# Gate vectors kept as columns and spread by transposes; matmul operands placed at one offset; 12 modulation chunks moved to VectorE

## The chip, the cores and the metric

The kernel runs on one core of one Trainium2 chip. The metric is device time in microseconds (us); lower is better. TensorE (PE in the profile) multiplies, VectorE (DVE) and ScalarE (ACT) work element by element, GpSimd (POOL) does a few powers, SyncE's queue (SP) starts most transfers. On-chip operands lie in SBUF, matmul results in PSUM.

## The reference, cut to what matters

Two streams of 128 tokens (a context stream, s = 0, and a latent stream, s = 1; width 2048) go through two layers. A layer computes six modulation vectors of 2048 from a conditioning vector, with a 2048 x 12288 weight matrix, and uses them around attention and a squared-ReLU MLP:

```python
sh_a, sc_a, gt_a, sh_m, sc_m, gt_m = split(silu(c) @ w_ada[l] + b_ada[l], 6)
h = rms_norm(x, g_pre_a) * (1.0 + sc_a) + sh_a
o = attention_heads(h @ w_in[l]) @ w_out[l]
x = x + gt_a * rms_norm(o, g_post_a)
h = rms_norm(x, g_pre_m) * (1.0 + sc_m) + sh_m
x = x + gt_m * rms_norm(square(relu(h @ w_up[l])) @ w_down[l], g_post_m)
```

Everything is float32. The weights are about 590 MB, read once. Both streams use the same weights; their modulation vectors differ.

## The kernel before, in words

**Weights and their split.** Weights come in chunks of 1 MB ([128, 2048] floats) into five `raw` buffers. For a matmul of the trunk ("t" chunk: w_in, w_out, w_up, w_down) each half of a chunk is split into a high part `wh` (ACT, L1031) and a low part `wl` (DVE, L1032, `split_to`), with three buffers each, two halves ahead of use. The activations are split likewise. Each product is then three matmuls in the fast 32-bit form: high by high, low by high, high by low. In `Group` (L364 to L366: w_in, w_out, w_down) the activation is stationary and 512 weight columns move; in `UpGroup` (L399 to L401: w_up, 128 chunks in all, 48 matmuls each) the weight is stationary and 256 activation columns move. Four PSUM accumulators are shared by both. The stationary activation is `XT0` to `XT3` for w_in and `big` for w_out and w_down.

**Modulation chunks.** The modulation weights are 1 MB chunks too, in one of two layouts. "ada" chunks go to TensorE (`ada_mm`, L150: four matmuls by 32 columns at once, each as two instructions); four chunks make one block of 512 outputs, which ACT copies (L154), TensorE transposes (L121, four of them on the tile `pt`) and DVE reduces (L167). "dv" chunks go to VectorE (`dv_mul`, L205): two products with a broadcast copy of silu(c), one for each stream (`sB`), each with a running sum of 2048 elements; four chunks make a block. The tables `DV_BLOCKS` and `PE_BLOCKS` say which blocks go where: before, layer 0 has 4 blocks on VectorE (the MLP gate, `G_M`) and 18 blocks, and two more in halves, on TensorE: 80 chunks, all in the first stage (w_in and w_out of layer 0, about 0 to 505 us). The 64 dv chunks that run beside the MLP of layer 0 and the 28 later ones make the 92 of the profile.

**Order.** `items` is a list written by the program: trunk chunks, with ada and dv chunks woven between them (`weave`). SP starts the transfers in about that order, as `raw` buffers come free (`issue`, L1018); a scheduler then orders each engine's instructions and may move one ahead of others that the program wrote earlier, unless `behind` forbids it. In the trace before, DVE takes dv products ahead of low parts written before them, and waits for their transfers.

**Gates.** A finished gate block (16 in all: two gates, two layers, four blocks) goes through `gate_fin`: it is written into a 32-column tile `gt`, four matmuls (L234, eight instructions) turn its columns into rows, ACT and DVE split these into `gc`. When a gate is needed, `gate_bc` spreads a block over 128 partitions by one matmul with a selector (`sv`, L301). It is called 32 times: two gates, two layers, two streams, four blocks; ACT (L879) or DVE (L954) reads the result.

**Addresses.** A pool lays its tiles out one behind the other, in the order in which their names are first asked for. `const` comes first, then `wp` (`raw`, `wh`, `wl`: all of 4 or 8 KB), then `sp`, which begins with five `big` of 8 KB, then `cT` of 128 bytes, then `tmp` (2 KB), `XT0` to `XT3` (8 KB each), small tiles, `stg`. So `raw`, `wh`, `wl` and `big` have one offset within 2 KB, and `XT` lies 128 bytes further.

Of the kernel before, what the change touches and what calls it, by code (L numbers as in the profile page):

```python
# [29 lines left out]
NACC = 4  # L30
TAIL = 4


G_A, G_M = [(2, b) for b in range(4)], [(5, b) for b in range(4)]
M_A = [(i, f) for f in range(4) for i in range(2)]
M_M = [(3 + i, f) for f in range(4) for i in range(2)]
DV_BLOCKS = [G_M, M_A + M_M[:4] + G_A[:3] + G_M]
PE_BLOCKS = [M_A[2:] + G_A + M_M, M_M[4:] + G_A[3:]]

C_ID, C_GC, C_GS, C_DC, C_DS, C_MK, C_LO, C_SV, C_END = 0, 128, 256, 384, 448, 512, 576, 577, 833


def _consts():
    c = np.zeros((P, C_END), np.float32)
    c[:, C_ID:C_ID + P] = np.eye(P, dtype=np.float32)
    for g in range(4):
        for v in range(2):  # L50
            for r in (v, 2 + v):
                c[32 * g + r, C_SV + P * v:C_SV + P * (v + 1)] = 1.0
            c[32 * g + 2 + v, C_LO] = -1.0
# [19 lines left out]
def trunk(ctx: ExitStack, tc: tile.TileContext, I, O):  # L73
    nc = tc.nc
    pe, act, dve, pool = nc.tensor, nc.scalar, nc.vector, nc.gpsimd

    const = ctx.enter_context(tc.tile_pool(name="const", bufs=1))
    wp = ctx.enter_context(tc.tile_pool(name="wp", bufs=1))
    sp = ctx.enter_context(tc.tile_pool(name="sp", bufs=1))
# [3 lines left out]
    def sb(shape, tag, bufs=1, dt=F32):  # L83
        return sp.tile(shape, dt, tag=tag, bufs=bufs, name=tag)

    def psm():
        return ps.tile([P, 512], F32, tag="m", bufs=7 - NACC, name="m")

    cs = const.tile([P, C_SV], F32, name="cs")
    ident = cs[:, C_ID:C_ID + P]  # L90
    sv = const.tile([P, 2 * P], F32R, name="sv")
    x = [None, None]
    xd = [I["xp"], I["xs"]]
    sT = const.tile([P, KT, 32], F32, name="sT")
    baT = const.tile([P, L, 96], F32, name="baT")
    ngT = const.tile([P, L, 4, KT], F32, name="ngT")
    hf = const.tile([P, 8], F32, name="hf")
    mods = [[const.tile([P, KT, 2], F32, name=f"mod{l}_{i}") for i in range(4)] for l in range(L)]
    biasB = const.tile([P, 4, P], F32, name="biasB")
# [17 lines left out]

    mark = {"pt": None, "res": None, "xt": None}

# [3 lines left out]
    def startup():  # L123
        for s in range(2):
            x[s] = sb([P, D], "big", 5)
            nc.sync.dma_start(x[s], xd[s])
        cT = sb([P, 2, KT], "cT")
        nc.scalar.dma_start(cT, I["cT"])
        nc.scalar.dma_start(cs, I["consts"][:, 0:C_SV])
        svf = sb([P, 512], "tmp", NTMP)  # L130
        nc.scalar.dma_start(svf[:, 0:2 * P], I["consts"][:, C_SV:C_END])
        nc.scalar.dma_start(baT, I["baT"])
        nc.scalar.dma_start(ngT, I["ngT"])
        dve.memset(sT, 0.0)
        dve.memset(hf, -0.5)
        for v in range(2):
            act.activation(sT[:, :, v], cT[:, v, :], AF.Silu)
        act.activation(sv, svf[:, 0:2 * P], AF.Copy)

# [16 lines left out]

    gcs = {}
    made = set()

    def ada_post(l, sec, blk, pt, j0, nj):  # L160
        yield
        m = psm()
        for j in range(nj):
            tr(m[:, j * P:(j + 1) * P], pt[:, j * P:(j + 1) * P])
        yield
        red = st1[:, 0:2 * nj].rearrange("p (j v) -> p j v", v=2)
        dve.tensor_reduce(red, m[:, 0:nj * P].rearrange("p (j g c) -> p j c g", g=4, c=32)[:, :, 0:2, :], AX.X,  # L167
                          ALU.add)
        if sec in (2, 5):
            yield from gate_fin(l, sec, blk, red)  # L170
        else:
            mod_fin(l, sec, blk, red, j0, nj)
# [20 lines left out]
    def load_sb():  # L193
        for v in range(2):
            nc.sync.dma_start(sB[v], I["crow"][v:v + 1, :].to_broadcast([P, D]))
        for v in range(2):
            act.activation(sB[v], sB[v], AF.Silu)

    def dv_mul(l, sec, blk, j, raw, release):
# [3 lines left out]
        for v in range(2):  # L203
            o = raw if v else sb([P, D], "junk", 1, FP8)
            p = dve.scalar_tensor_tensor(o, raw, 1.0, sB[v], ALU.mult, ALU.mult, accum_out=a[:, j, v:v + 1],  # L205
                                         saturate=None if v else False)
            behind(p, mark["xt"])
            if v:
                release()
            yield  # L210
        if j == 3:
            if sec in (2, 5):
                yield from gate_fin(l, sec, blk, a)
            else:
                mod_fin(l, sec, blk, a)

    def gate_fin(l, sec, blk, red):

        w = 0 if sec == 2 else 1
        gt = sb([P, 4, 32], "gt")  # L220
        dve.memset(gt, 0.0)
        k0 = 4 * blk
        for v in range(2):
            dve.tensor_tensor(gt[:, :, v], red[:, :, v], baT[:, l, 16 * sec + k0:16 * sec + k0 + 4], ALU.add)
            dve.tensor_tensor(gt[:, :, v], gt[:, :, v], ngT[:, l, 2 * w + 1, k0:k0 + 4], ALU.mult)
        dve.tensor_copy(gt[:, :, 2:4], gt[:, :, 0:2])
        if (l, w) not in gcs:
            gcs[(l, w)] = sb([P, 512], "gc", dt=F32R)
        gc = gcs[(l, w)]
        yield  # L230
        m = psm()
        r = slice(32 * blk, 32 * blk + 32)
        for j in range(4):
            pe.matmul(m[r, j * P:(j + 1) * P], gt[:, j, :], ident, start=True, stop=True,  # L234
                      tile_position=(0, 32 * blk))
        yield
        h = sb([P, 512], "tmp", NTMP, F32R)
        act.activation(h[r, :], m[r, :], AF.Copy)
        dve.scalar_tensor_tensor(gc[r, :], h[r, :].bitcast(F32), cs[r, C_LO:C_LO + 1], m[r, :], ALU.mult, ALU.add)
        made.add((l, w, blk))  # L240
# [54 lines left out]

    def gate_bc(l, w, s, n):
        m = psm()
        gc = gcs[(l, w)]
        assert (l, w, n) in made
        r = slice(32 * n, 32 * n + 32)  # L300
        pe.matmul(m, sv[r, P * s:P * (s + 1)], gc[r, :], start=True, stop=True,  # L301
                  tile_position=(32 * n, 0))
        return m
# [482 lines left out]
    for l in range(L):  # L786
# [41 lines left out]
        if l == 0:  # L828
            items.insert(0, ("call", startup))
            fill, dv = ada_items(0, G_A + M_M), []  # L830
            h0 = lambda h: [("ada", I["w_ada0"][sec, h, kq], (0, sec, 0, kq, h)) for sec in range(2) for kq in range(4)]
# [9 lines left out]
            items.extend(a1[:2] + m[3:4] + a1[2:4] + m[4:5] + a1[4:6] + m[5:6] + a1[6:] + m[6:7])  # L841
            xt(1)
            items.extend(m[7:])
            for f in range(1, 4):
                ch = [c for cg in cG for c in cg[2 * f:2 * f + 2]]
                if f == 1:
                    call(lambda l=l: layer_consts(l))
                if f < 3:
                    weave(ch[:5], ada_items(0, M_A[2 * f + 2:2 * f + 4]))
                    items.append(ch[5])  # L850
                    xt(f + 1)
                    items.extend(ch[6:])
                else:
                    weave(ch, fill[:8])
            weave(c2, fill[8:16])
            rest, fill = [], fill[16:]
        else:
# [165 lines left out]
    def split_to(k):  # L1023
        while state["split"] <= min(k, len(subs) - 1):
# [136 lines left out]
```

## Time and profile before

| what | us |
|---|---|
| median of 3 runs (2336.02 to 2344.62) | 2338.56 |
| the profiled execution's own time | 2343.01 |
| its span, first to last instruction | 2340.9 |
| PE busy, of the span | 2272.9 |
| DVE busy | 1613.8 |
| ACT busy | 1100.9 |

The profiled execution is one run with a profile; durations are read from it. PE rows are matmuls as the profile models their ends: consecutive ones overlap, so the rate is read from the distance between starts, not from the duration of one. PEclk in the profile is the granted clock, a share of full speed.

### The profile page before, as it was taken

How to read it: one execution, taken by the hardware profiler on the slowest of the kernel's cores; microseconds unless marked ns; L12 is line 12 of the kernel's file. 1: busy time of each engine (PE TensorE's matmuls, PEld its weight loads, DVE VectorE, ACT ScalarE, POOL GpSimd, SP SyncE). 2: the span in 40 equal slices, each digit the busy share in tenths (PEclk: the TensorE clock that was granted, in tenths of full speed). 3: DMA queues.
4: the chain of work that ended last, by engine and by line, in shares of the span. 5: the costliest groups of instructions: out<-in, count | busy, mean ns of one | idle time of the engine just before them, and what ended most of it. 6: DMA issues, size and time to landing. Idle time of an engine off the chain costs nothing.

```text
span 2340.9 us, 33080 instructions
## 1 busy us (share of the span) xinstructions
PE 2272.9 (97%) x13480; PEld 1901.3 (81%) x13480; DVE 1613.8 (69%) x2028; ACT 1100.9 (47%) x1525; POOL 21.8 (1%) x30
## 2 busy tenths in 40 slices
PE   6999999989999999999999999998999999999998
PEld 3567666779889889889877777877989988988986
DVE  2565755489888998998758688547566566565545
ACT  4334444465444445435445455546544444543543
POOL 0000000000000000000000000000000000000000
PEclk9999999999999999999999999999999999999999
DMA  8888777887877777787857665665666566565552
GB/s 325 301 321 335 289 302 303 338 285 294 307 273 296 291 290 289 275 298 279 338 185 274 247 242 197 240 241 209 216 232 220 200 230 216 201 223 210 192 183 90
DMA packets 92496, 601.35 MB, mean 257 GB/s; under 512 B 13752, under 2 KB 16184, under 8 KB 21432
## 3 DMA queue, kind: packets, MB, share of 16 engines
q1 hardware_dynamic: 91624, 598.64, 69.2%
q8 instruction: 105, 1.72, 0.3%
q10 hardware_dynamic: 720, 0.61, 0.1%
q14 instruction: 47, 0.39, 0.0%
HBM read 591.61 MB, written 7.60 MB: 256 GB/s over the span
## 4 chain that ended last, share of the span: by engine, by line
PE 87%; DVE 6%; DMA 2%; issue 2%; ACT 2%; POOL 1%; ACTq 0%; POOLq 0%; DVEq 0%
PE acc L364 16%; PE acc L365 16%; PE acc L366 16%; PE acc L401 10%; PE acc L400 10%; PE acc L399 10%; PE ada L150 4%; DVE wl L1032 3%; PE m L121 2%; DMA raw<-w_adaT_in 2%; PE m L487 1%; PE m L234 1%; POOL st L108 1%; DMA raw<-w_in_in 0%; DVE raw L205 0%
## 5 line engine op out<-in xcount | busy, mean ns | idle before, releaser
L1031 ACT ACTIVATE wh<-raw 128x1024 fp32r<-128x1024 f32 x720 | 759.0, 1059 | 918.0 <-PE acc L366 548.6
L1032 DVE TENSOR_TENSOR wl<-raw,wh 128x1024 fp32r<-128x1024 f32 x720 | 874.7, 1223 | 418.7 <-ACT wh L1031 416.3
L401 PE MATMUL acc<-XT,wl 128*128 128x256 f32 x2048 | 580.3, 284 | 2.5 <-DVE wl L1032 2.5
L399 PE MATMUL acc<-XT,wh 128*128 128x256 f32 x2048 | 577.3, 282 | 2.5 <-ACT XT L277 2.5
L400 PE MATMUL acc<-XT,wh 128*128 128x256 f32 x2048 | 579.4, 283 | 0.3 <-DVE XT L278 0.3
L364 PE MATMUL acc<-wh,big 128*128 128x512 f32 x1280 | 502.0, 394 | 0.0
L365 PE MATMUL acc<-wl,big 128*128 128x512 f32 x1280 | 500.2, 391 | 1.7 <-DVE wl L1032 1.7
L366 PE MATMUL acc<-wh,big 128*128 128x512 f32 x1280 | 498.7, 390 | 0.0
L399 PEld LDWEIGHTS acc<-XT,wh 128*128 128x128 f32 x2048 | 387.5, 189 | 4.0 <-ACT XT L277 3.1
L401 PEld LDWEIGHTS acc<-XT,wl 128*128 128x128 f32 x2048 | 386.5, 189 | 3.8 <-DVE wl L1032 3.6
L400 PEld LDWEIGHTS acc<-XT,wh 128*128 128x128 f32 x2048 | 386.0, 188 | 0.8 <-DVE XT L278 0.5
L364 PEld LDWEIGHTS acc<-wh,big 128*128 128x128 f32 x1280 | 240.1, 188 | 61.5 <-issue 9.2
L365 PEld LDWEIGHTS acc<-wl,big 128*128 128x128 f32 x1280 | 240.5, 188 | 52.0 <-DVE wl L1032 3.4
L366 PEld LDWEIGHTS acc<-wh,big 128*128 128x128 f32 x1280 | 240.4, 188 | 50.5 <-issue 0.5
L364 PE MATMUL acc<-wh,XT 128*128 128x512 f32 x576 | 230.6, 411 | 9.9 <-ACT wh L1031 6.5
L205 DVE SCALAR_TENSOR_TENSOR junk<-raw,sB 128x2048 fp8e5<-128x2048 f32 x92 | 210.5, 2288 | 36.5 <-DMA raw<-w_adaT_in 36.4
L365 PE MATMUL acc<-wl,XT 128*128 128x512 f32 x576 | 229.7, 399 | 1.6 <-DVE wl L1032 1.2
L366 PE MATMUL acc<-wh,XT 128*128 128x512 f32 x576 | 228.0, 396 | 0.0
L205 DVE SCALAR_TENSOR_TENSOR raw<-raw,sB 128x2048 f32<-128x2048 f32 x92 | 210.4, 2287 | 0.0
L364 PEld LDWEIGHTS acc<-wh,XT 128*128 128x128 f32 x576 | 108.5, 190 | 51.1 <-ACT wh L1031 12.2
L365 PEld LDWEIGHTS acc<-wl,XT 128*128 128x128 f32 x576 | 109.0, 189 | 31.3 <-DVE wl L1032 6.5
L366 PEld LDWEIGHTS acc<-wh,XT 128*128 128x128 f32 x576 | 108.8, 189 | 24.5 <-issue 0.2
(134 smaller groups left out, 1225.1 us busy)
## 6 DMA issues: line engine op xcount, KB each, us to landing
raw<-w_up_in SPq DMA_DIRECT2D x128, 1024.0 KB, 5.6
raw<-w_down_in SPq DMA_DIRECT2D x128, 1024.0 KB, 5.0
raw<-w_adaT_in SPq DMA_DIRECT2D x92, 1024.0 KB, 4.9
raw<-w_ada_in SPq DMA_DIRECT2D x80, 1024.0 KB, 6.3
raw<-w_in_in SPq DMA_DIRECT2D x72, 1024.0 KB, 5.8
raw<-w_out_in SPq DMA_DIRECT2D x32, 1024.0 KB, 4.8
XT<-w_ada_in SPq DMA_DIRECT2D x12, 1024.0 KB, 7.4
raw<-w_ada_in SPq DMA_DIRECT2D x16, 512.0 KB, 5.1
```

The costliest lines, as they stand in the source:

```text
L108: pool.tensor_tensor(out, out, hf[:, 0:width], ALU.pow)
L121: pe.transpose(out, in_, ident)
L150: pe.matmul(pa[32 * g:32 * g + 32, 0:w], sT[:, 4 * kq + g, :], raw[:, g * w:(g + 1) * w], start=(kq == 0), stop=(kq == 3), tile_position=( ...
L205: p = dve.scalar_tensor_tensor(o, raw, 1.0, sB[v], ALU.mult, ALU.mult, accum_out=a[:, j, v:v + 1], saturate=None if v else False)
L364: pe.matmul(a, xh, wh[:, c], start=first, stop=False)
L365: pe.matmul(a, xh, wl[:, c], start=False, stop=False)
L366: pe.matmul(a, xl, wh[:, c], start=False, stop=last)
L399: pe.matmul(a, wh[:, c], xh, start=first, stop=False)
L400: pe.matmul(a, wh[:, c], xl, start=False, stop=False)
L401: pe.matmul(a, wl[:, c], xh, start=False, stop=last)
L1031: act.activation(wh, r, AF.Copy)
L1032: behind(dve.tensor_tensor(wl, r, wh.bitcast(F32), ALU.subtract), mark["res"])
```

## The change

Three parts, in the words of the code. Gates: `gate_fin` writes a block into the columns of one `gates[w]` tile, [128, 16, 2], with two additions and two products and nothing on TensorE; `gate_bc` makes four transposes (L121's helper) of one such column, repeated 128 times by a step of zero. `gt`, `gc`, `sv`, the selector constants and their copy at the start are gone. Addresses: a pool `lead` (512 bytes and three times 128) stands first, then `wp`, then a new pool `op` with `big`, `XT`, `stg` and `tmp`, then the constants, then the rest. Chunks: blocks G_A[0], G_A[1] and the last of M_M of layer 0 (12 chunks) become dv chunks in the first stage; `sB` is loaded there, and every dv product and every low part, in both layers, is chained behind the one written before it.

```diff
+OPERANDS = ("big", "XT0", "XT1", "XT2", "XT3", "stg", "tmp")
-DV_BLOCKS = [G_M, M_A + M_M[:4] + G_A[:3] + G_M]
-PE_BLOCKS = [M_A[2:] + G_A + M_M, M_M[4:] + G_A[3:]]
+DV_BLOCKS = [G_A[:2] + M_M[7:] + G_M, M_A + M_M[:4] + G_A[:3] + G_M]
+PE_BLOCKS = [M_A[2:] + G_A[2:] + M_M[:7], M_M[4:] + G_A[3:]]
...
+    lead = ctx.enter_context(tc.tile_pool(name="lead", bufs=1))
+    wp = ctx.enter_context(tc.tile_pool(name="wp", bufs=1))
+    op = ctx.enter_context(tc.tile_pool(name="op", bufs=1))
     const = ctx.enter_context(tc.tile_pool(name="const", bufs=1))
-    wp = ctx.enter_context(tc.tile_pool(name="wp", bufs=1))
     sp = ctx.enter_context(tc.tile_pool(name="sp", bufs=1))
...
-        return sp.tile(shape, dt, tag=tag, bufs=bufs, name=tag)
+        pl = op if tag in OPERANDS else sp
+        return pl.tile(shape, dt, tag=tag, bufs=bufs, name=tag)
...
-    ngT = const.tile([P, L, 4, KT], F32, name="ngT")
+    ngT = lead.tile([P, L, 4, KT], F32, name="ngT")
-    mods = [[const.tile([P, KT, 2], F32, name=f"mod{l}_{i}") for i in range(4)] for l in range(L)]
+    mods = [[(lead if 4 * l + i < 3 else const).tile([P, KT, 2], F32, name=f"mod{l}_{i}") for i in range(4)]
+            for l in range(L)]
...
+    def chain(inst):
+        behind(inst, mark["dve"])
+        mark["dve"] = inst
...
-        nc.scalar.dma_start(cs, I["consts"][:, 0:C_SV])
-        svf = sb([P, 512], "tmp", NTMP)
-        nc.scalar.dma_start(svf[:, 0:2 * P], I["consts"][:, C_SV:C_END])
+        nc.scalar.dma_start(cs, I["consts"])
...
-        act.activation(sv, svf[:, 0:2 * P], AF.Copy)
...
+    gates = [const.tile([P, KT, 2], F32, name=f"gate{w}") for w in range(2)]
...
     def load_sb():
         for v in range(2):
             nc.sync.dma_start(sB[v], I["crow"][v:v + 1, :].to_broadcast([P, D]))
+
+    def silu_sb():
         for v in range(2):
-            act.activation(sB[v], sB[v], AF.Silu)
+            behind(act.activation(sB[v], sB[v], AF.Silu), mark["wh"])
...
             behind(p, mark["xt"])
+            chain(p)
...
     def gate_fin(l, sec, blk, red):
         w = 0 if sec == 2 else 1
-        gt = sb([P, 4, 32], "gt")
-        dve.memset(gt, 0.0)
         k0 = 4 * blk
         for v in range(2):
-            dve.tensor_tensor(gt[:, :, v], red[:, :, v], baT[:, l, 16 * sec + k0:16 * sec + k0 + 4], ALU.add)
-            dve.tensor_tensor(gt[:, :, v], gt[:, :, v], ngT[:, l, 2 * w + 1, k0:k0 + 4], ALU.mult)
-        dve.tensor_copy(gt[:, :, 2:4], gt[:, :, 0:2])
...
-        for j in range(4):
-            pe.matmul(m[r, j * P:(j + 1) * P], gt[:, j, :], ident, start=True, stop=True,
-                      tile_position=(0, 32 * blk))
...
-        act.activation(h[r, :], m[r, :], AF.Copy)
-        dve.scalar_tensor_tensor(gc[r, :], h[r, :].bitcast(F32), cs[r, C_LO:C_LO + 1], m[r, :], ALU.mult, ALU.add)
+            o = gates[w][:, k0:k0 + 4, v]
+            dve.tensor_tensor(o, red[:, :, v], baT[:, l, 16 * sec + k0:16 * sec + k0 + 4], ALU.add)
+            dve.tensor_tensor(o, o, ngT[:, l, 2 * w + 1, k0:k0 + 4], ALU.mult)
...
     def gate_bc(l, w, s, n):
         m = psm()
-        gc = gcs[(l, w)]
         assert (l, w, n) in made
-        r = slice(32 * n, 32 * n + 32)
-        pe.matmul(m, sv[r, P * s:P * (s + 1)], gc[r, :], start=True, stop=True,
-                  tile_position=(32 * n, 0))
+        for j in range(4):
+            tr(m[:, j * P:(j + 1) * P], gates[w][:, 4 * n + j, s:s + 1].to_broadcast([P, P]))
         return m
...
-            fill, dv = ada_items(0, G_A + M_M), []
+            fill, dv = ada_items(0, G_A[2:] + M_M[:7]), dv_items(0, G_A[:2] + M_M[7:])
...
             xt(1)
+            call(load_sb)
             items.extend(m[7:])
+            call(lambda l=l: layer_consts(l))
...
                 if f == 1:
-                    call(lambda l=l: layer_consts(l))
+                    call(silu_sb)
+                    weave(ch[:5], ada_items(0, M_A[2 * f + 2:2 * f + 4]), dv[:2])
+                if f == 2:
+                    weave(ch[:5], ada_items(0, M_A[2 * f + 2:2 * f + 4]), dv[2:4])
...
-                    weave(ch, fill[:8])
-            weave(c2, fill[8:16])
-            rest, fill = [], fill[16:]
+                    weave(ch, fill[:8], dv[4:8])
+            weave(c2, fill[8:12])
+            rest, fill, dv = [], fill[12:], dv[8:]
...
-        cut = 0 if l == 0 else 40
+        cut = 10 if l == 0 else 40
...
-            act.activation(wh, r, AF.Copy)
-            behind(dve.tensor_tensor(wl, r, wh.bitcast(F32), ALU.subtract), mark["res"])
+            mark["wh"] = act.activation(wh, r, AF.Copy)
+            p = dve.tensor_tensor(wl, r, wh.bitcast(F32), ALU.subtract)
+            behind(p, mark["res"])
+            chain(p)
```

## Rows read from the trace of the kernel before

**Rows 1.** The page: engines (busy us, share, count) and the chain's shares.

```profile
PE 2272.9 (97%) x13480; PEld 1901.3 (81%) x13480; DVE 1613.8 (69%) x2028; ACT 1100.9 (47%) x1525; POOL 21.8 (1%) x30
...
PE 87%; DVE 6%; DMA 2%; issue 2%; ACT 2%; POOL 1%; ACTq 0%; POOLq 0%; DVEq 0%
```

**Rows 2.** Windows: stretch, its length, busy of each engine, PEclk, DMA share, GB/s.

```profile
130.00:400.00 270.00, 264.97 (x1383) 182.81 (x1375) 164.95 (x313) 122.54 (x215) 6.31 (x5) 1.00 0.81 311
505.00:1222.00 717.00, 712.82 (x4539) 645.11 (x4538) 623.36 (x638) 328.77 (x372) 0.00 (x0) 1.00 0.77 286
```

**Rows 3.** Timeline of PE, 172 us: two ada chunks between matmuls (start, length, instruction).

```profile
171.97 0.40 PE L366 MATMUL acc<-wh,XT 128*128 128x512 f32 x1
...
172.30 1.92 PE L150 MATMUL ada<-raw,sT 128*32 128x512 f32 x16
174.15 0.49 PE L364 MATMUL acc<-wh,XT 128*128 128x512 f32 x1
174.49 0.39 PE L365 MATMUL acc<-wl,XT 128*128 128x512 f32 x1
```

**Rows 4.** Timeline of PE, 177 us: four transposes of a modulation block.

```profile
176.81 0.39 PE L366 MATMUL acc<-wh,XT 128*128 128x512 f32 x1
177.05 0.60 PE L121 MATMUL m<-cs,pt 128*128 128x128 f32 x4
177.40 0.47 PE L364 MATMUL acc<-wh,XT 128*128 128x512 f32 x1
```

**Rows 5.** Timeline of PE, 683 us: the matmuls of one gate block.

```profile
683.00 0.28 PE L401 MATMUL acc<-XT,wl 128*128 128x256 f32 x1
683.21 1.06 PE L234 MATMUL m<-cs,gt 128*32 128x128 f32 x8
684.20 0.39 PE L399 MATMUL acc<-XT,wh 128*128 128x256 f32 x1
```

**Rows 6.** Timeline of PE, 1170 us: one spreading of a gate block.

```profile
1169.65 0.39 PE L366 MATMUL acc<-wh,big 128*128 128x512 f32 x1
1169.97 0.50 PE L301 MATMUL m<-gc,sv 32*128 32x512 f32 x1
1170.40 0.50 PE L364 MATMUL acc<-wh,big 128*128 128x512 f32 x1
```

**Rows 7.** Timeline of PE, 1700 us: first and last of 55 matmuls, stationary `big`.

```profile
1699.65 0.39 PE L366 MATMUL acc<-wh,big 128*128 128x512 f32 x1
...
1711.89 0.39 PE L366 MATMUL acc<-wh,big 128*128 128x512 f32 x1
```

**Rows 8.** Timeline of PE, 1257 us: first and last of 12 matmuls, stationary `XT1`.

```profile
1256.64 0.40 PE L364 MATMUL acc<-wh,XT 128*128 128x512 f32 x1
...
1259.19 0.39 PE L366 MATMUL acc<-wh,XT 128*128 128x512 f32 x1
```

**Rows 9.** Timeline of PE, 1691 us: first, last two of 48 matmuls of w_up.

```profile
1690.77 0.28 PE L399 MATMUL acc<-XT,wh 128*128 128x256 f32 x1
...
1696.23 0.28 PE L400 MATMUL acc<-XT,wh 128*128 128x256 f32 x1
1696.34 0.28 PE L401 MATMUL acc<-XT,wl 128*128 128x256 f32 x1
```

**Rows 10.** The page's groups: line, operation, count, busy us, mean ns, idle before.

```profile
L1031 ACT ACTIVATE wh<-raw 128x1024 fp32r<-128x1024 f32 x720 | 759.0, 1059 | 918.0 <-PE acc L366 548.6
L1032 DVE TENSOR_TENSOR wl<-raw,wh 128x1024 fp32r<-128x1024 f32 x720 | 874.7, 1223 | 418.7 <-ACT wh L1031 416.3
...
L205 DVE SCALAR_TENSOR_TENSOR junk<-raw,sB 128x2048 fp8e5<-128x2048 f32 x92 | 210.5, 2288 | 36.5 <-DMA raw<-w_adaT_in 36.4
...
L364 PE MATMUL acc<-wh,XT 128*128 128x512 f32 x576 | 230.6, 411 | 9.9 <-ACT wh L1031 6.5
```

**Rows 11.** Timeline of ACT at the start: the selector's copy and its wait.

```profile
10.80 0.42 ACT L138 ACTIVATE sv<-tmp 128x256 fp32r<-128x256 f32 x1 [3.22 <-DMA tmp<-consts_in]
```

**Rows 12.** The view of the tile `sB`: its loads (count, issue ns, first and last start).

```profile
L195 SPq DMA_DIRECT2D sB<-crow_in x2: 423/586/748, 209.7 to 219.3; - x2
```

More of the change, by code (lines that the diff above doesn't have):

```diff
@@ L36 @@
 M_M = [(3 + i, f) for f in range(4) for i in range(2)]
-DV_BLOCKS = [G_M, M_A + M_M[:4] + G_A[:3] + G_M]
-PE_BLOCKS = [M_A[2:] + G_A + M_M, M_M[4:] + G_A[3:]]
-C_ID, C_GC, C_GS, C_DC, C_DS, C_MK, C_LO, C_SV, C_END = 0, 128, 256, 384, 448, 512, 576, 577, 833
+DV_BLOCKS = [G_A[:2] + M_M[7:] + G_M, M_A + M_M[:4] + G_A[:3] + G_M]
+PE_BLOCKS = [M_A[2:] + G_A[2:] + M_M[:7], M_M[4:] + G_A[3:]]
+C_ID, C_GC, C_GS, C_DC, C_DS, C_MK, C_END = 0, 128, 256, 384, 448, 512, 576
 def _consts():
@@ L48, in _consts @@
     c[:, C_ID:C_ID + P] = np.eye(P, dtype=np.float32)
[L49 to L53, printed above, removed]
     t = np.arange(P)
@@ L83, in sb @@
     def sb(shape, tag, bufs=1, dt=F32):
-        return sp.tile(shape, dt, tag=tag, bufs=bufs, name=tag)
+        pl = op if tag in OPERANDS else sp
+        return pl.tile(shape, dt, tag=tag, bufs=bufs, name=tag)
     def psm():
         return ps.tile([P, 512], F32, tag="m", bufs=7 - NACC, name="m")
-    cs = const.tile([P, C_SV], F32, name="cs")
+    cs = const.tile([P, C_END], F32, name="cs")
     ident = cs[:, C_ID:C_ID + P]
-    sv = const.tile([P, 2 * P], F32R, name="sv")
     x = [None, None]
@@ L115, in behind @@
                               reason="issue order")
-    mark = {"pt": None, "res": None, "xt": None}
+    mark = {"pt": None, "res": None, "xt": None, "dve": None, "wh": None}
+    def chain(inst):
+        behind(inst, mark["dve"])
+        mark["dve"] = inst
     def tr(out, in_):
@@ L155, in ada_mm @@
             fast.append(ada_post(l, sec, blk, pt, 0 if half is None else 2 * half, w // P))
-    gcs = {}
+    gates = [const.tile([P, KT, 2], F32, name=f"gate{w}") for w in range(2)]
     made = set()
@@ L169, in ada_post @@
         if sec in (2, 5):
-            yield from gate_fin(l, sec, blk, red)
+            gate_fin(l, sec, blk, red)
         else:
@@ L212, in dv_mul @@
             if sec in (2, 5):
-                yield from gate_fin(l, sec, blk, a)
+                gate_fin(l, sec, blk, a)
             else:
@@ L219, in gate_fin @@
         w = 0 if sec == 2 else 1
-        gt = sb([P, 4, 32], "gt")
-        dve.memset(gt, 0.0)
         k0 = 4 * blk
         for v in range(2):
-            dve.tensor_tensor(gt[:, :, v], red[:, :, v], baT[:, l, 16 * sec + k0:16 * sec + k0 + 4], ALU.add)
-            dve.tensor_tensor(gt[:, :, v], gt[:, :, v], ngT[:, l, 2 * w + 1, k0:k0 + 4], ALU.mult)
-        dve.tensor_copy(gt[:, :, 2:4], gt[:, :, 0:2])
-        if (l, w) not in gcs:
-            gcs[(l, w)] = sb([P, 512], "gc", dt=F32R)
-        gc = gcs[(l, w)]
-        yield
-        m = psm()
-        r = slice(32 * blk, 32 * blk + 32)
-        for j in range(4):
-            pe.matmul(m[r, j * P:(j + 1) * P], gt[:, j, :], ident, start=True, stop=True,
-                      tile_position=(0, 32 * blk))
-        yield
-        h = sb([P, 512], "tmp", NTMP, F32R)
-        act.activation(h[r, :], m[r, :], AF.Copy)
-        dve.scalar_tensor_tensor(gc[r, :], h[r, :].bitcast(F32), cs[r, C_LO:C_LO + 1], m[r, :], ALU.mult, ALU.add)
+            o = gates[w][:, k0:k0 + 4, v]
+            dve.tensor_tensor(o, red[:, :, v], baT[:, l, 16 * sec + k0:16 * sec + k0 + 4], ALU.add)
+            dve.tensor_tensor(o, o, ngT[:, l, 2 * w + 1, k0:k0 + 4], ALU.mult)
         made.add((l, w, blk))
@@ L297, in gate_bc @@
         m = psm()
-        gc = gcs[(l, w)]
         assert (l, w, n) in made
-        r = slice(32 * n, 32 * n + 32)
-        pe.matmul(m, sv[r, P * s:P * (s + 1)], gc[r, :], start=True, stop=True,
-                  tile_position=(32 * n, 0))
+        for j in range(4):
+            tr(m[:, j * P:(j + 1) * P], gates[w][:, 4 * n + j, s:s + 1].to_broadcast([P, P]))
         return m
@@ L846, in trunk @@
                 if f == 1:
-                    call(lambda l=l: layer_consts(l))
+                    call(silu_sb)
+                    weave(ch[:5], ada_items(0, M_A[2 * f + 2:2 * f + 4]), dv[:2])
+                if f == 2:
+                    weave(ch[:5], ada_items(0, M_A[2 * f + 2:2 * f + 4]), dv[2:4])
                 if f < 3:
-                    weave(ch[:5], ada_items(0, M_A[2 * f + 2:2 * f + 4]))
                     items.append(ch[5])
@@ L970, in trunk @@
         if l + 1 < L:
-            rest.insert(1, ("call", load_sb))
             g, m = dv_items(0, G_M), dv_items(1, M_A + M_M[:4])
             dv = [x for i in range(16) for x in m[3 * i:3 * i + 3] + g[i:i + 1]]
-            weave(rest[:4], [])
-            weave(rest[4:119], [], dv)
+            weave(rest[:3], [])
+            weave(rest[3:118], [], dv)
             call(lambda: drain_dv())
             call(lambda l=l: layer_consts(l + 1))
-            items.extend(rest[119:])
+            items.extend(rest[118:])
             items.extend(ada_items(1, G_A[3:]))
```

## The prediction

> **What bounds the kernel now.** The page comes first: PE is busy 97% of the span, and 87% of the chain that ended last is PE work; DVE, transfers and ACT share the rest [rows 1]. [...] So PE is the limit nearly everywhere, and an instruction taken from its queue is worth the time by which it pushed its neighbours apart. A matmul's own duration doesn't give that (they overlap), so the prices below are distances between starts in the timeline. [...]
>
> **Chunks taken from PE.** Two ada chunks between trunk matmuls: from the matmul ahead of them to the one behind, 174.15 - 171.97 = 2.18 us, where the usual step is 0.23; the step after is 0.34, 0.11 too long [rows 3]. That is 2.06 us a pair, and 12 chunks are 6 pairs: 12.4 us. Each of the 3 blocks also loses four transposes: 177.40 - 176.81 - 0.23 = 0.36 us [rows 4], 1.1 us together.
>
> **Gates.** A gate block pushes its neighbours apart by 684.20 - 683.00 - 0.12 = 1.08 us [rows 5]; 16 blocks, 17.3 us, all gone, since additions into columns need no PE. Spreading a block costs 1170.40 - 1169.65 - 0.23 = 0.52 us now [rows 6] and four transposes 0.36 [rows 4]: 32 times 0.16, 5.1 us. No row shows a transposed operand with a step of zero. Below, I see no reason for less than the 0.36; above, if it took twice that, the 32 spreadings would cost 11.5 us more; I take 0.36, since the same 128 columns are loaded. ACT and DVE lose a copy and a few small instructions per block, which no one waits for. PE saves 12.4 + 1.1 + 17.3 + 5.1 = 35.9 us.
>
> **Addresses.** This part has a price in the trace, because two placements are in it already. With `big` stationary, at the same offset within 2 KB as the moving weights, 54 steps take 12.24 us: 0.2267 each [rows 7]. With `XT` stationary, 128 bytes off, 11 steps take 2.55 us: 0.2318, and uneven [rows 8]. Instruction, columns and clock are the same. After the change all are at one offset, so I expect 0.2267 for the 3 x 576 matmuls on `XT` [rows 10]: 1728 x 5.1 ns = 8.8 us; ends 0 and twice that. In w_up `XT` moves and `wh` or `wl` is stationary, also 128 bytes apart, at 5.57 us for 47 steps, 0.1185 [rows 9]. No row shows that pair at one offset. [...] From below: single steps read 0.11 [rows 9], under 0.115; at 0.115 they save 6144 x 3.5 ns = 21.5 us. I take the nearest row, no change. `big` keeps its relation: 0.
>
> [...]
>
> **The start.** ACT waits 3.22 us for the selector constants and copies them for 0.42 [rows 11], with the first squares behind it in its queue. Both go. The modulation's first copy comes later on the same queue; but the first weights may not have landed any sooner. I take 1.5 us of 3.6, ends 0 and 3.6.
>
> **Work added to DVE, and its order.** 12 chunks are 24 products of 2.29 us [rows 10]: 55 us more in a stage where DVE has, at the rate of rows 2, some 39% free. Behind a product in DVE's queue wait the low parts (PE's operands, two halves ahead), the additions that free PSUM accumulators and the softmax steps. Were each product exposed, 55 us; beside the MLP of layer 0, 64 such chunks leave PE idle 4.2 us in all [rows 2], 0.07 a chunk, 0.8 us for 12. Accumulators are drained more often in the first stage: I take 3 us lost. `sB` is loaded at 209.7 and 219.3 us [rows 12], so inside the first stage already; the two loads, SP's constants for the layer and the two ACT copies of it only come earlier in it, among transfers that use 0.81 of the time: 0, at worst two landings of a few us with PE idle. The chain fixes DVE's order in both MLPs. Before, products taken ahead waited 36.4 us for their transfers [rows 10], but PE lost only those 4.2 us, so the chain can win 4; I count 0.
>
> **The sum.** 35.9 + 8.8 + 1.5 - 3 = 43.2 us. The profiled execution took 2343.0, 4.4 more than the median of the runs: 2343.0 - 43.2 - 4.4 = 2295.4, forecast 2295.
>
> **The rivals.**
> [...]
> *w_up gains as well*, its steps settle at the shortest seen: 2295 - 21 = 2274. For it: these steps are uneven, so something in them varies; against: no row says that one offset picks the short ones.
> *The raw buffers starve.* An ada chunk frees its buffer after 1 us of PE; a dv chunk holds it for two products in order, at least 4.58 us, of only five buffers. If PE then waits the difference for each, 12 x 3.6 = 43 us and the gain is gone: 2338. Against: transfers have 0.19 of their time free.
> *DVE becomes the limit beside the MLP of layer 0: slower.* DVE is idle there 717 - 623 = 94 us. Low parts wait for the high part, whose copy takes 1.06 us [rows 10]; before, products written later filled such waits, and the chain forbids it. The stretch has 256 halves: from 0.37 us idle per half on, DVE decides, and at the full 1.06 us it needs 623 + 271 = 894 us, 177 more: 2472. Against it: the copies run two halves ahead, so DVE waits only when it is ahead of PE.
> [...]
>
> **Chances.** Forecast 0.48 (its own range 2275 to 2312: zero steps at double price, w_up up by 9, DVE's cost 0 to 10), placement worth nothing 0.20, w_up gains 0.17, starving 0.07, DVE the limit 0.05, every matmul faster 0.03. Under 0.5%, 11.7 us, a change can't be told from none here. Faster: 0.48 + 0.20 + 0.17 + 0.03 = 0.88; within 0.5%: 0.07; slower: 0.05. The range goes from 2258 (w_up at 0.115, `XT` twice its price) to 2318 (forecast with the zero steps at double price and 9 us more in w_up), leaving out starving, DVE the limit and the last rival.
>
> **What would show it.** L234 and L301 gone; four transposes, 0.36 us between neighbours, in the place of L301; 104 rather than 92 products of each of the two kinds on DVE, and 68 rather than 80 transfers of whole ada chunks into `raw`. w_in steps of 0.227, w_up steps of 0.1185 or else. The first stage (chunks, a gate's 4 blocks and 8 spreadings, half of the 8.8, the start, less 3) should end some 22 us earlier, the MLP of layer 0 (4 blocks, 8 spreadings) shorten by 5 to 6. Wrong if PE's busy share falls under 96% in either window of rows 2, or if steps on `XT` stay at 0.232.

## The result, and the profile after

The changed kernel takes 2374.67 us (median of 4 runs, 2371.44 to 2376.17) against 2339.79 before: ratio 1.0145 (95% interval 1.0126 to 1.0163). It is 35 us slower (34 by the ratio); 2295 was forecast, 43 us faster than the 2338.56 on record then.

The page after: engines (busy us, share, count) and the chain's shares, to set beside [rows 1].

```profile
PE 2265.7 (96%) x13340; PEld 1907.6 (81%) x13340; DVE 1647.8 (70%) x2025; ACT 1083.0 (46%) x1503; POOL 24.4 (1%) x30
...
PE 75%; DVE 11%; DMA 7%; ACT 3%; issue 3%; POOL 1%; POOLq 0%; ACTq 0%; DVEq 0%; SPq 0%
```

PE has 7 us less work in a span 29 us longer, and its share of the chain falls from 87 to 75%; DVE and transfers take its place. The windows say where (columns as in [rows 2], whose stretches are the first two):

```profile
130.00:400.00 270.00, 249.43 (x1242) 173.98 (x1240) 199.59 (x327) 108.67 (x194) 6.31 (x5) 0.99 0.81 306
505.00:1222.00 717.00, 701.31 (x4507) 635.27 (x4508) 618.23 (x636) 324.45 (x382) 0.00 (x0) 1.00 0.75 279
...
400.00:505.00 105.00, 93.86 (x482) 63.26 (x480) 53.65 (x100) 44.29 (x83) 2.22 (x4) 0.93 0.74 281
```

PE idles 20.6 us in the first stretch (5.0 before) and 15.7 in the second (4.2); in the third, 400 to 505 us, it is busy 93.86 us at a granted clock of 0.93 (98.02 at 0.98 before). Its share is 92% in the first, which the prediction had named as the sign that it is wrong.

The same trunk matmul, found in both traces, gives a ledger by stage. Both kernels issue 11712 trunk matmuls in nearly one order; the k-th start of one is set against the k-th of the other, each from the start of its own span:

| trunk matmul | before, us | after, us | difference | forecast |
|---|---|---|---|---|
| first | 27.0 | 24.4 | -2.6 | -1.5 |
| first of w_up's second chunk, layer 0 | 497.2 | 515.8 | +18.7 | -22 |
| near the end of layer 0's MLP | 1198.3 | 1232.2 | +33.9 | -28 |
| last | 2329.1 | 2356.5 | +27.3 | -43 |

So the first stage loses 21 us from its first matmul on, the MLP of layer 0 another 15; layer 1 gains 7.

**What holds the MLP back.** Waits in 505 to 1222 us, in the kernel before and then after (who waits <- for whom: us in total, times, longest us; other lines left out):

```profile
DVE junk L205 <- DMA raw<-w_adaT_in: 23.5, 21, 2.3
...
PEld acc L401 <- DVE wl L1032: 3.3, 4, 1.4
PEld acc L365 <- DVE wl L1032: 2.8, 3, 1.6
```

```profile
ACT wh L1022 <- DMA raw<-w_down_in: 123.6, 39, 7.4
ACT wh L1022 <- DMA raw<-w_up_in: 93.5, 33, 6.6
...
PEld acc L389 <- DVE wl L1023: 11.7, 15, 1.6
PEld acc L353 <- DVE wl L1023: 10.4, 18, 2.2
```

Before, no split waited for a trunk transfer there; DVE waited 23.5 us for weights of products that it took early. Now the splits wait 217 us, and the weight loads' waits for `wl` (PEld, which overlaps PE) rise from 6.1 to 22.1 us. The transfers into `raw` are not slower (median from issue to landing in 700 to 800 us: 5.6 us before, 4.8 after): they start late. The timelines of SP's queue and of DVE after, around 710 us (start, length, instruction; other rows left out), show why:

```profile
702.19 0.33 SPq L1009 DMA_DIRECT2D raw<-w_adaT_in  x1
...
711.79 0.33 SPq L1009 DMA_DIRECT2D raw<-w_adaT_in  x1
718.64 0.33 SPq L1009 DMA_DIRECT2D raw<-w_up_in  x1
724.80 0.33 SPq L1009 DMA_DIRECT2D raw<-w_adaT_in  x1
```

```profile
718.53 2.28 DVE L208 SCALAR_TENSOR_TENSOR junk<-raw,sB 128x2048 fp8e5<-128x2048 f32 x1
...
722.48 2.29 DVE L208 SCALAR_TENSOR_TENSOR raw<-raw,sB 128x2048 f32<-128x2048 f32 x1
724.69 0.08 DVE L208 DVE_READ_ACCUMULATOR raw<-raw,sB 128x1 f32 x1
...
728.10 2.29 DVE L208 SCALAR_TENSOR_TENSOR junk<-raw,sB 128x2048 fp8e5<-128x2048 f32 x1
```

Products come in the order of their transfers. The chunk asked for at 702.19 gets its first product at 728.10, 25.9 us later. The one whose products start at 718.53 and 722.48 had been asked for at 691.6; at 724.69 its buffer comes free, held for 33 us, and 0.11 us later SP starts the next transfer. A new dv chunk is asked for every 11 us or so, and 33 / 11 = 3: three of the five buffers are with dv chunks. The kernel before, at the same place:

```profile
703.23 0.33 SPq L1018 DMA_DIRECT2D raw<-w_adaT_in  x1
...
714.27 0.33 SPq L1018 DMA_DIRECT2D raw<-w_adaT_in  x1
```

```profile
708.59 2.29 DVE L205 SCALAR_TENSOR_TENSOR junk<-raw,sB 128x2048 fp8e5<-128x2048 f32 x1 [0.40 <-DMA raw<-w_adaT_in]
...
711.95 2.28 DVE L205 SCALAR_TENSOR_TENSOR raw<-raw,sB 128x2048 f32<-128x2048 f32 x1
```

Asked for at 703.23, first product at 708.59, free at 714.2: 11 us, one buffer. The scheduler took products the moment their weights landed, ahead of low parts written earlier; that is the reordering the chain forbids. Over 600 to 1100 us the median from issue to first product is 5.2 to 5.6 us in each 100 us before and 23.5 to 25.3 after, and from issue to the end of the second product, when the buffer comes free, 11.0 to 12.5 before and 29.4 to 32.4 after; for trunk chunks, from issue to split, 14.6 to 16.0 before and 5.8 to 6.4 after, where 4.8 is the landing itself. Hardly any slack is left.

**What holds the first stage back.** PE's timeline after, around 115 us, with the idle time ahead of an instruction and its releaser in brackets, and SP's queue in the same stretch:

```profile
112.92 0.66 PE L125 MATMUL m<-cs,pt 128*128 128x128 f32 x4 [0.72 <-ACT pt L155]
119.41 1.22 PE L352 MATMUL acc<-wh,XT 128*128 128x512 f32 x2 [5.83 <-ACT wh L1022]
120.67 0.79 PE L353 MATMUL acc<-wl,XT 128*128 128x512 f32 x1
121.26 0.63 PE L354 MATMUL acc<-wh,XT 128*128 128x512 f32 x1
121.69 0.63 PE L353 MATMUL acc<-wl,XT 128*128 128x512 f32 x1
```

```profile
84.94 0.33 SPq L1009 DMA_DIRECT2D raw<-w_adaT_in  x1
90.56 0.33 SPq L1009 DMA_DIRECT2D raw<-w_in_in  x1
90.93 0.90 SPq L196 DMA_DIRECT2D sB<-crow_in  x2
...
107.28 0.92 SPq L695 DMA_DIRECT2D rpbz<-cv  x1
108.30 0.52 SPq L1009 DMA_DIRECT2D raw<-w_in_in  x1
```

The w_in chunk for which PE waits 5.83 us was asked for at 108.30, is split from 118.3, and followed the previous one (90.56) by 18 us. Between them lie 2 MB of `sB` and the layer's constants: `rpbz` reads what a transfer of 98.49 brings, and the queue stands 6.9 us for it. The kernel before has the constants at nearly the same time (5.3 us of standing, chunks of w_in at 88.90 and 103.15), so of these only `sB` is new. New, too, is an `adaT` chunk that has held its buffer since 84.94; its first product starts at 122.3. The 13 dv chunks asked for before 505 us hold their buffers for 35 to 69 us. After the idle PE steps by 0.43 us rather than 0.227: the granted clock is 0.50 in 118 to 122 us. Over the span it is 0.985 on average against 0.995; an estimate from these means and the two levels that both traces have, 1.00 and 0.50, is 0.015 x 2 x 2369.5 = 71 us at the lower level against 23. From matmul 216 to matmul 288 of the ledger, 104 to 135 us, the changed kernel loses 8.0 of the 21 us; the rest goes in smaller places, which were not followed one by one.

**What came out as said.** Four transposes of a gate column: 1211.02 - 1210.44 - 0.23 = 0.35 us [rows 4]; the zero step costs nothing.

```profile
1210.44 0.39 PE L354 MATMUL acc<-wh,big 128*128 128x512 f32 x1
1210.67 0.60 PE L125 MATMUL m<-cs,gate 128*128 128x128 f32 x4
1211.02 0.48 PE L352 MATMUL acc<-wh,big 128*128 128x512 f32 x1
```

Steps on `XT` are 2.49 / 11 = 0.2264 us, as forecast [rows 8]; those of w_up 2.16 / 18 = 0.120, where the forecast left them at 0.1185, and now even [rows 9]. First and last of 12 and of 19 matmuls, from PE's timeline at 107 and 710 us:

```profile
107.05 0.39 PE L353 MATMUL acc<-wl,XT 128*128 128x512 f32 x1
...
109.54 0.39 PE L354 MATMUL acc<-wh,XT 128*128 128x512 f32 x1
```

```profile
709.72 0.28 PE L387 MATMUL acc<-XT,wh 128*128 128x256 f32 x1
...
711.88 0.28 PE L387 MATMUL acc<-XT,wh 128*128 128x256 f32 x1
```

### The profile page after: what moved, and what is told of

Same layout as the page of the kernel before. It is cut to its first block, busy times and chain, and to the rows that moved or that the text cites. A ratio compares the mean times of both kernels' runs of the same rounds, so it can differ in the third digit from the quotient of the medians.

```text
span 2369.5 us, 32796 instructions
## 1 busy us (share of the span) xinstructions
PE 2265.7 (96%) x13340; PEld 1907.6 (81%) x13340; DVE 1647.8 (70%) x2025; ACT 1083.0 (46%) x1503; POOL 24.4 (1%) x30
## 4 chain that ended last, share of the span: by engine, by line
PE 75%; DVE 11%; DMA 7%; ACT 3%; issue 3%; POOL 1%; POOLq 0%; ACTq 0%; DVEq 0%; SPq 0%
PE acc L353 14%; PE acc L354 14%; PE acc L352 14%; PE acc L389 9%; PE acc L388 9%; PE acc L387 9%; DVE wl L1023 5%; DMA raw<-w_down_in 3%; PE ada L151 3%; PE m L125 2%; ACT wh L1022 2%; DMA raw<-w_up_in 2%; DVE raw L208 2%; DVE junk L208 1%; DMA raw<-w_in_in 1%
## 5 line engine op out<-in xcount | busy, mean ns | idle before, releaser
L1023 DVE TENSOR_TENSOR wl<-raw,wh 128x1024 fp32r<-128x1024 f32 x720 | 873.3, 1222 | 464.7 <-ACT wh L1022 463.4
L389 PEld LDWEIGHTS acc<-XT,wl 128*128 128x128 f32 x2048 | 393.1, 192 | 11.8 <-DVE wl L1023 11.7
L387 PEld LDWEIGHTS acc<-XT,wh 128*128 128x128 f32 x2048 | 393.8, 192 | 4.0 <-ACT XT L266 3.2
L388 PEld LDWEIGHTS acc<-XT,wh 128*128 128x128 f32 x2048 | 394.2, 192 | 0.7 <-DVE XT L267 0.6
L353 PEld LDWEIGHTS acc<-wl,big 128*128 128x128 f32 x1280 | 241.3, 189 | 61.8 <-DVE wl L1023 13.6
L208 DVE SCALAR_TENSOR_TENSOR junk<-raw,sB 128x2048 fp8e5<-128x2048 f32 x104 | 237.5, 2284 | 0.0
L208 DVE SCALAR_TENSOR_TENSOR raw<-raw,sB 128x2048 f32<-128x2048 f32 x104 | 237.5, 2284 | 0.0
L352 PE MATMUL acc<-wh,XT 128*128 128x512 f32 x576 | 223.0, 409 | 15.0 <-ACT wh L1022 9.5
L354 PE MATMUL acc<-wh,XT 128*128 128x512 f32 x576 | 228.3, 397 | 0.0
L353 PEld LDWEIGHTS acc<-wl,XT 128*128 128x128 f32 x576 | 110.0, 191 | 42.3 <-DVE wl L1023 17.4
```

Source lines behind the costliest of these rows:

```text
L352: pe.matmul(a, xh, wh[:, c], start=first, stop=False)
L353: pe.matmul(a, xh, wl[:, c], start=False, stop=False)
L354: pe.matmul(a, xl, wh[:, c], start=False, stop=last)
L387: pe.matmul(a, wh[:, c], xh, start=first, stop=False)
L388: pe.matmul(a, wh[:, c], xl, start=False, stop=False)
L389: pe.matmul(a, wl[:, c], xh, start=False, stop=last)
```

## The experiments

Ratios are to the kernel before, measured beside each on the same chip (medians 2341.7 to 2344.4), with 95% intervals. How much a stage ends late, or shortens, is read against the kernel before from the ledger's matmuls; in the runs' texts "the weight loads wait" stands for the PEld lines of 505 to 1222 us.

**1. Without the chain.** Both calls of `chain` go; all else as changed.

```diff
             behind(p, mark["xt"])
-            chain(p)
...
             behind(p, mark["res"])
-            chain(p)
```

> The changed kernel without the chain on VectorE (both calls gone); gates, placement and the 12 chunks stay. Theory A (the chain makes the products late, so each holds its raw buffer some 25 us instead of some 5 to 10, and the trunk's chunks land too late): nearly all of the loss goes, time 2290 to 2310, products start about 5 us after their transfer is issued in the MLP of layer 0. Theory B (the 12 chunks' own work on VectorE delays low parts and accumulators in the first stage): only the MLP's part goes, 2350 to 2360. Theory C (gates by transposes or the placement slow TensorE): 2365 to 2380.

2338.66 us, 0.9977 [0.9966, 0.9987], in none of the three ranges: most of the loss goes, and more was expected to. The MLP of layer 0 shortens by 6.6 us against before, where 15 were lost with the chain: the forecast's 5 to 6. No split waits for a trunk transfer there. The first stage still ends 4.3 us late, rather than 18.7; its dv chunks hold their buffers for 10 to 30 us.

**2. The 12 chunks back on TensorE, chain kept.**

```diff
-DV_BLOCKS = [G_A[:2] + M_M[7:] + G_M, M_A + M_M[:4] + G_A[:3] + G_M]
-PE_BLOCKS = [M_A[2:] + G_A[2:] + M_M[:7], M_M[4:] + G_A[3:]]
+DV_BLOCKS = [G_M, M_A + M_M[:4] + G_A[:3] + G_M]
+PE_BLOCKS = [M_A[2:] + G_A + M_M, M_M[4:] + G_A[3:]]
...
```

> The changed kernel with the 12 chunks back on TensorE; chain, gates and placement stay. Theory A: the first stage has no products to hold buffers and recovers, the MLP of layer 0 keeps its loss of some 20 us: 2325 to 2340. Theory B: all of the loss goes, 2305 to 2315. Theory C: 2375 to 2390.

2354.09 us, 1.0041 [1.0027, 1.0055], again in none of the ranges. The first stage ends 3.1 us early, the MLP still loses 16; its splits wait 213 us for trunk transfers. So the MLP's loss needs the chain and not the 12 chunks, and these, too, cost time.

**3. The kernel before with the chain alone.** The two calls and `chain` itself added to it.

> The kernel before with nothing but the chain. Theory A: slower, 2355 to 2370, the MLP of layer 0 some 20 us longer and its trunk chunks used about 6 us after issue instead of 15. Theories B and C: 2335 to 2345.

2371.34 us, 1.0114 [1.0095, 1.0134], 1 us over the range of its first theory: most of the loss, without gates, placement or chunks. Nothing is lost by the end of the first stage (-1.8), 29.7 us in the MLP of layer 0, where 64 dv chunks pass, and 0.6 behind it, where 28 do. In the changed kernel the chain costs that MLP 22 us (the ledger against run 1's); why it is less there was not found. Its waits in 505 to 1222 us:

```profile
ACT wh L1036 <- DMA raw<-w_down_in: 149.7, 48, 7.7
ACT wh L1036 <- DMA raw<-w_up_in: 103.3, 33, 7.0
...
PEld acc L406 <- DVE wl L1037: 18.3, 24, 1.9
PEld acc L370 <- DVE wl L1037: 13.5, 22, 2.3
```

**4. Chain kept, products written at once** rather than spread behind low parts, so that a buffer is held for less time.

```diff
-            while len(dvq) > 2:
+            while dvq:
                 step_list(dvq, 1)
```

> The changed kernel, chain kept, but each dv chunk's products are written at once where the chunk stands in the list, not up to two chunks later. Theory A: buffers are held shorter by about two trunk chunks (some 10 us), a large part of the loss goes: 2310 to 2345. Theory B: 2370 or more, the same work in front of the low parts. Theory C: no change, 2370 to 2380.

2368.48 us, 1.0103 [1.0087, 1.0119]: little is won, a miss for buffers as the only cause. From issue to first product it is 18 us rather than 25, to the buffer's release some 22 rather than 31, and late trunk transfers are gone; but both products now stand in a row ahead of low parts, and the weight loads wait 30 us for these:

```profile
PEld acc L389 <- DVE wl L1023: 15.8, 14, 2.1
PEld acc L353 <- DVE wl L1023: 14.3, 18, 1.9
...
ACT wh L1022 <- DMA raw<-w_down_in: 2.2, 1, 2.2
```

**5. The same with one product at a time.** The queue of written products is one deep, and the rule for emptying it moves along.

```diff
-            while len(dvq) > 2:
+            while len(dvq) > 1:
...
-state["credit"] += 0.5 + 0.5 * (len(dvq) > 1)
+state["credit"] += 0.5 + 0.5 * (len(dvq) > 0)
```

> The changed kernel, chain kept, with at most one dv chunk waiting and one product after each half chunk (before: two chunks, half a product on average). Theory A: a dv chunk holds its buffer some 15 us rather than 25, products are not bunched, the MLP of layer 0 loses at most 8 us against the kernel before: time 2345 to 2360. Rival D: 2368 or more, as when both products were written at once.

2345.76 us, 1.0015 [1.0006, 1.0024]. From issue to first product it is 19 us, to the release 25, and the weight loads wait 3.3 us for `wl`; the MLP shortens by 5.8 us. So a written order can cost twice, by buffers held and by late low parts, and this one avoids most of both.

**6. A sixth raw buffer, chain and chunks kept.** Room comes from a third `tmp`, a second `qT` and an eighth `st2`.

```diff
-NRAW = 5
+NRAW = 6
-NTMP = 3
+NTMP = 2
...
```

> The changed kernel, chain kept, with six raw buffers rather than five (to make room: two tmp buffers rather than three, one qT rather than two, seven small statistics tiles rather than eight, which may cost the attention stages a little). Theory A (buffers held too long): ACT's waits for trunk transfers beside the MLP of layer 0 fall from 217 us to under 60, that stage loses at most 6 us against the kernel before, not 15; time 2345 to 2362. Rival D (the order alone: products stand in front of low parts, whatever the buffers): the stage keeps its 15 us or more, time 2368 to 2385.

2329.25 us, 0.9942 [0.9929, 0.9955], 16 us under the range of its first theory. With the same order, and 33 to 35 us from issue to release, the waits for trunk transfers in 505 to 1222 us fall from 217 to 13 us, and the MLP of layer 0 shortens by 7.2:

```profile
ACT wh L1022 <- DMA raw<-w_up_in: 10.1, 3, 4.1
...
ACT wh L1022 <- DMA raw<-w_down_in: 3.1, 1, 3.1
...
PEld acc L353 <- DVE wl L1023: 1.7, 7, 0.3
```

**7. Gates and placement alone** (edits 1 and 2 together; the early `sB` loads stay).

> The changed kernel without the chain and with the 12 chunks on TensorE: gates and placement alone. By the terms of the prediction 29 us under before at its full price (ratio 0.987); by the stages of the two runs so far (first stage 3, MLP of layer 0 7, layer 1 8) 18 us (ratio 0.992). If gates or placement cost something: 1.00 or more.

2327.49 us, 0.9942 [0.9930, 0.9953]: less than either of the two gains expected.

**8. Placement alone, in the kernel before.** The pools `lead` and `op` and the new order, nothing else.

> The kernel before with the placement alone. If the step depends on the operands' offsets as the rows of the changed kernel show: 0.227 on XT (1728 matmuls, 9 us won), 0.120 in w_up (some 3 us lost), ratio 0.997. If the steps came from something else: 0.232 stays, ratio 1.000.

2341.07 us, 0.9996 [0.9987, 1.0004]. The first stage ends 6.0 us early, the MLP of layer 0 takes 3.6 longer, the rest is level: the gain on `XT` is in good part handed back in w_up.

**9 to 11. The sixth buffer in the other three.** With edit 6: the 12 chunks on TensorE and the chain kept; no chain and the chunks on VectorE; neither.

> The changed kernel with its chain, with a sixth raw buffer, and the 12 chunks back on TensorE. Beside it stand two kernels already run: the same with five buffers 2354.1, the same with five buffers and no chain 2327.5. Theory A (the chain costs time only because two of five buffers are held some 20 us longer): with six, ACT's waits for trunk transfers beside the MLP of layer 0 fall from 213 us to under 10 and the time to 2323 to 2330, level with the kernel without the chain. Rival O (the written order itself costs, since low parts then wait behind products): the 26.6 us between those two remain for the most part, 2342 to 2350, with DVE late for PE (waits for wl over 15 us) and no late transfers.

> The changed kernel without the chain and with a sixth raw buffer; the 12 chunks stay on VectorE. With five buffers it took 2338.7, and with the 12 chunks on TensorE 2327.5. Theory B (the 12 chunks cost their 6.6 to 11 us in the first stage because a chunk for VectorE holds one of five buffers for over 20 us while the trunk's transfers are on the limit): the sixth buffer gives that back, 2325 to 2331. Rival F (the matmuls taken from PE there only filled waits for transfers that the bandwidth sets, and the rest is the half clock after the waits): the buffer changes little, 2335 to 2340, and the first stage ends as late as with five.

> Gates and placement alone (no chain, the 12 chunks on TensorE) with a sixth raw buffer; with five it took 2327.5. Theory A: five buffers are enough where nothing holds them longer, PE never waits for a transfer beside the MLP of layer 0; within 4 us of the kernel with five, 2323 to 2330. Rival R (a sixth buffer is worth some 20 us in any version, so that what it gave the changed kernel says nothing of the chain): 2300 to 2312.

They took 2318.06, 2324.01 and 2321.56 us. With runs 1, 2, 6 and 7 this fills a square (ratio to before; intervals for the new ones 0.9872 to 0.9908, 0.9897 to 0.9935, 0.9886 to 0.9925):

| | chunks on TensorE | chunks on VectorE |
|---|---|---|
| five buffers, no chain | 0.9942 | 0.9977 |
| five buffers, chain | 1.0041 | 1.0145 |
| six buffers, no chain | 0.9906 | 0.9916 |
| six buffers, chain | 0.9890 | 0.9942 |

With five buffers the chain costs 1.0 to 1.7%; with six nothing on the left, 0.3% on the right. That ends the rival of run 9, that the order costs by itself there: the weight loads wait 2.2 us for `wl`, and the splits 13 for trunk transfers. The time is 5 us under the range of its first theory. The chunks cost 0.35% with five buffers and no chain; with six their difference, 2.45 us, lies within the intervals, so run 10, 1 us under the range of its first theory, supports the theory of the buffers. Run 11 ended 1.4 us under the range of its own: the sixth buffer is worth some 6 to 8 us to a kernel without chain or chunks (by the medians, by the ratios), against 45 to 48 to the changed one.

**12. The early loads put back**, on run 9's kernel: `sB` after the first chunk of w_up, the constants one group of w_in later.

```diff
-            call(load_sb)
             items.extend(m[7:])
-            call(lambda l=l: layer_consts(l))
...
                 if f == 1:
-                    call(silu_sb)
+                    call(lambda l=l: layer_consts(l))
...
+            rest.insert(1, ("call", lambda: (load_sb(), silu_sb())))
```

> The kernel with chain, six raw buffers and the 12 chunks on TensorE (2318.1, ratio 0.989), with the two loads of sB, their ACT copies and the layer's constants put back to where the kernel before had them (sB just after the first chunk of w_up, the constants one group of w_in later). Theory S (the early loads cost time: in every kernel that has them the trunk loses 2.4 to 8.3 us between its matmuls 144 and 288, about 84 to 135 us, and the one with placement alone loses none there): the loss of 3.9 us there goes, the first stage ends some 4 us earlier, 2313 to 2315, ratio about 0.987. Rival T (that loss has another cause, the gates' or the weights' own; the forecast's price of 0 for the loads holds): 2317 to 2321.

2315.98 us, 0.988 [0.9864, 0.9897], between the two ranges. The time as a whole is 2 us lower, and the intervals overlap, so the answer lies in the stretch that the loads were moved out of. Windows of 85 to 136 us, run 9 and then run 12 (columns as in [rows 2]; before: PE 49.31, clock 1.00):

```profile
85.00:136.00 51.00, 48.16 (x208) 32.23 (x207) 28.96 (x45) 19.74 (x23) 0.00 (x0) 0.93 0.85 309
```

```profile
85.00:136.00 51.00, 50.28 (x246) 33.55 (x244) 30.18 (x51) 18.75 (x24) 0.00 (x0) 1.00 0.81 295
```

Without the loads an idle of 2.08 us and the steps of 0.43 us behind it (0.23 ahead of it) are gone, and the first stage ends 5.2 us earlier. The constants were not moved in effect: SP starts them at 96.4 us in both. So `sB` is what costs there, by its loads or by the two ACT copies that moved with them. The timelines of ACT and of PE in run 9 speak for the copies, one of which stands straight ahead of the split that PE waits for:

```profile
112.48 1.90 ACT L200 ACTIVATE sB<-sB 128x2048 f32<-128x2048 f32 x1
114.28 1.99 ACT L1022 ACTIVATE wh<-raw 128x1024 fp32r<-128x1024 f32 x2
```

```profile
115.38 1.22 PE L352 MATMUL acc<-wh,XT 128*128 128x512 f32 x2 [2.08 <-ACT wh L1022]
```

Loads and copies were not moved one without the other. This is the fastest of the kernels, level with run 9; both beat the kernel before and the changed one.

## Why the prediction was wrong

The step that failed is "The chain fixes DVE's order in both MLPs. Before, products taken ahead waited 36.4 us for their transfers [rows 10], but PE lost only those 4.2 us, so the chain can win 4; I count 0." The chain is a fourth part of the change, listed under the chunks. The step counted DVE's idle time and not what the early products bought: a raw buffer given back after 11 to 12 us instead of 29 to 32. Run 3 prices the chain at 27 us on the kernel before, run 1 at 39 in the changed one (0.0168 x 2342; by the ledger 15 in the first stage and 22 in the MLP), and run 6 shows the way: one buffer more, and all but some 6 us of it is gone (run 6 against run 10, whose intervals overlap). It is not the only step that failed: run 1, without the chain, gains 5 to 6 us where 43 were forecast. Gates, addresses and the start were to bring 32.7 us and brought 13.6 (run 7, with the early `sB` loads inside); the chunks were to bring 10.5 and, with five buffers, cost 8 or more. The rival of the starving buffers had the resource, with a chance of 0.07, but at the wrong place: it took "at least 4.58 us" as the hold of the 12 chunks alone, where the order decides the hold, and the 92 chunks of before stand in it too. The row was there to be read: issue to first product in the MLP of layer 0, and the buffers' turn in SP's queue.

- **Chunks, 12.4 + 1.1 + (-3).** PE lost work: with six buffers and no chain it is busy 2246.2 us rather than 2255.1 (runs 10 and 11). The time did not follow: in 24 to 505 us PE idles 30.4 us in run 10 and 21.6 in run 11, so what was taken from it came back as idle time. Without the chain the chunks cost 8 us with five buffers (0.0035 x 2342) and 2 with six; under the chain 24 and 12. In that stretch the splits wait 26.7 us for w_in transfers in run 10 and 10.0 in run 11; this fits that pairs of ada matmuls had filled PE's waits for transfers, which no run tried by itself. The 3 us for DVE's part were mis-sized as well, since DVE's queue was priced and the buffer was not. That the granted clock is lower around an idle of PE is seen in the windows of the changed kernel (5.83 us of idle, 0.50 in 118 to 122 us); how much of the 8 us is clock and how much is waiting was not parted, nor why 12 us remain under the chain with six buffers.
- **`sB` loads, 0.** Forecast as at worst two landings; run 12 gives 2 to 5 us, an idle of 2.08 us and steps of 0.43 us behind it. What was left out is ACT's queue: a copy of 1.90 us ahead of a split.
- **Gates, 17.3 + 5.1.** The price of each block holds (0.35 us for four transposes). Together they are worth 0.54%, 12.6 us, by runs 7 and 8, with the early `sB` loads inside; without the 2 to 5 us that run 12 gives for these, an estimate is 15 to 18. Some of the rest bought no time: three places near 468, 1222 and 1585 us that held such matmuls between waits take about as long as before (19.8, 15.4 and 16.6 us before; 19.8, 15.0 and 17.4 after). How much of the rest that is was not measured.
- **Addresses, 8.8.** The steps on `XT` came out where [rows 7] put them, those of w_up at 0.120, but the gain is nearly nothing: "I take the nearest row, no change" for w_up was the mis-sized term. Steps that nothing disturbs (under 0.3 us on `XT`, under 0.17 in w_up, both before and in run 8) can be set against each other one by one: 1555 on `XT` take 6.7 us less than before and 6080 of w_up 4.9 us more. The mean step goes from 0.2325 to 0.2282 on `XT` and from 0.1192 to 0.1200 in w_up; on `big`, whose relation stayed, from 0.2277 to 0.2278. No run shows the 9 us by which the ranges let w_up rise; the 4.9 us of run 8 stand in their place. Placement worth nothing, with a chance of 0.20, is right of run 8's time (0.9996) and wrong of the steps: 0.2318 became 0.2264. Every matmul faster, with 0.03, was not seen: the steps of w_up and `big` did not get shorter. What it is in the addresses that sets a step was not tried.
- **The start, 1.5.** It was 2.6 us.
- **DVE as the limit beside the MLP.** It didn't happen: DVE's busy time there fell from 623 to 618 us. The weight loads do wait for low parts (22.1 us against 6.1), but these are late because the splits ahead of them wait for transfers: in run 6 the same order leaves 2.3 us.
- **The range, 2258 to 2318.** The terms named for its ends give 2295 - 21.5 - 8.8 = 2265 and 2295 + 11.5 + 9 = 2316; the measured time is far outside either way, since both ends count the chain at 0.

The parts don't add up: gates and placement -13.6 us, chunks +8, chain +23 by runs 7, 1 and 2 make +18, and +34 was measured. Chunks and chain draw on the same five buffers.

## What to carry to other kernels

A written order on one engine also sets how long its inputs' buffers are held (here 29 to 32 us rather than 11 to 12): before fixing it, multiply the time from issue to release by the rate of such chunks, and compare the product with the number of buffers. Work taken off the busiest engine need not be worth its time: in run 10 PE was busy 8.9 us less than in run 11 and idle 8.8 us more in the first stage, where splits waited for transfers, so that it may have been filling the wait. Place operands by measured steps, for every pair at once: what one matmul form gains another can hand back (run 8: 6.7 us and 4.9).

## What the runs showed of the hardware

- A matmul's step changed with where its operands lie: 512 columns at 0.2264 us with both operands at one offset within 2 KB and 0.2318 at 128 bytes apart; 256 columns at an even 0.120 against 0.115 to 0.123 with a mean of 0.1192. Run 8, placement alone, shows both, while the steps on `big`, whose relation stayed, do not change (0.2277 and 0.2278).
- A transpose of one column repeated by a step of zero takes no longer than that of a full tile: 0.35 and 0.36 us for four.
- An idle of 5.83 us was followed by steps of 0.43 us at a granted clock of 0.50, rather than 0.227, so that this late transfer cost more than its wait; the 2.08 us of run 9 by ten steps of 0.427 us, with a mean clock of 0.93 in 85 to 136 us.
